# One transformer layer in split fp32: a smaller constant of exponents, and the left side of SBUF 64 bytes lower

## The chip, the core and the metric

The kernel runs on one core of a Trainium2 chip. The metric is the time of one execution on the device, in microseconds (us); several executions are timed, and their median counts. A second, profiled execution gives the trace from which all rows below are taken.

## What is computed

The reference is one layer of a diffusion backbone over 1024 latent tokens and 256 context tokens, 1024 channels wide, all in fp32. Cut to what matters here:

```
h   = x * (1 + scale1) + shift1                 # scale, shift, gate: silu(c) @ w_mod + b_mod
q_b = rope(qk_rms(h @ w_qb + b, q_norm_g))      # 8 heads of 64
qk_rms(t, g) = t * rsqrt(mean(t*t) + 1e-6) * g  # per head
k_b likewise (2 heads); q_a, k_a without qk_rms
o_a = windowed attention (+-128 tokens and the context, a sink per head)
o_b = global attention over 1024 + 256 keys
y   = (sigmoid(g_a) * (o_a @ w_a) + sigmoid(g_b) * (o_b @ w_b)) @ w_out
x   = LN(alpha * x + gate1 * y)
u   = conv3(modulate(x) @ w_up);  y = (silu(u_gate) * u_val) @ w_down     # 2816 wide
out = LN(alpha * x + gate2 * y)
```

## The kernel before

Products are split. An fp32 matrix is held as a high part (its fp32r rounding) and a low part (the rest), and `mm3` (L92 to L95) forms each product with three matmuls: high by high (L93), high by low and low by high (L94, L95). Nearly all have 512 moving columns; some have 256. On TensorE a matmul has a stationary operand of 128 columns and a moving one of up to 512. `split` makes the two parts: a cast on ACT, VectorE or GpSimd (L85, L87) and a subtraction (L90).

The stages, in the order of time: the query projection of branch B with the modulation (q1acc, to 70 us); the other projections and the gates (acc, g, to about 320 us); the two attentions, unit by unit (s: scores, ptr: transposes, av: values, and b, the branch products, between and behind them, to about 805 us); the output product y with the first normalization and the first columns of u (to 990 us); the up products in a seven-product scheme (a, b, c, d by `up_tile`, 990 to 1370 us); the down products in the same scheme (p, yl, yt, to the end). In the attention and after it the order on TensorE is that of the program's text, partly fixed by hand.

SBUF has two stacks of tiles. The left side begins with constants (`const`), then come `hp` (19 general slots of 4 KB, handed out by `ht` and taken back by `hput`) and, later, `opool` and `post`. The right side holds `ph1` and `hTp` in the first phase, and later `qp`, `att`, `wq` and `za` (the last adds sixteen general slots to those of `hp`). So in the later stages an operand from `ht` may lie on either side, and a weight from the rings `w` (pool `wq`) on the right and `wd` (pool `post`) on the left.

The constants are laid one behind the other, and the last of them is `mhalf` (L118), 24 columns of -0.5, that is 96 bytes a partition. It is the exponent of all reciprocal square roots, which GpSimd takes as a power: for the keys (L303, 2 columns), for two tiles of queries at once (L355 in `qstats`, 16 columns, four times between 70 and 126 us), in the normalizations (L1102, 4 or 2 columns) and in the last one (L1678, 1 column). `pqs` and `nqs`, the scales of the queries, are [128, 8 tiles, 8 heads] in the constant `cvt`; they are read again in the attention of branch B, from 460 us on.

Where tiles lie, by the program's own allocation, as the byte address in a partition modulo 512 (tiles and the pieces of them that matmuls read are a whole number of 512 bytes long, so a pool's tiles share the value):

| tiles | before | after |
|---|---|---|
| `ident`, `identr` and all constants ahead of `mhalf` | unchanged | unchanged |
| left: `hp` slots, `opool` (O), `post` (raw, wd) | 288 | 224 |
| right, first phase: weights, hh, hl | 352 | 352 |
| right, later: q1, q2, ring w, `za` slots, maskr | 480 | 480 |
| right, attention: pth, ptl | 224 | 224 |
| right, attention: p | 96 | 96 |

The moving operand is the activation (hh, B, T, O, mh, pth) in most stages; in q1acc, acc and p it is the weight, and in s the key.

Of the kernel before, what the change touches and what calls it, by code (L numbers as in the profile page):

```python
# [7 lines left out]
F32 = mybir.dt.float32  # L8
R32 = mybir.dt.float32r
AF = mybir.ActivationFunctionType  # L10
ALU = mybir.AluOpType
AX = mybir.AxisListType

P = 128
# [56 lines left out]
def layer_kernel(  # L71
# [6 lines left out]
    nc = tc.nc  # L78
# [20 lines left out]
    def ctile(shape, dt, name):  # L99
        return const.tile(shape, dt, tag=name, name=name)  # L100
# [14 lines left out]
    pqs, nqs = (cvt[:, n * 64:n * 64 + 64].rearrange("p (a b) -> p a b", b=8) for n in (0, 1))  # L115
    onec = ctile([P, 1], F32, "onec")
    onesf = ctile([P, P], F32, "onesf")
    mhalf = ctile([P, 24], F32, "mhalf")  # L118
    nc.vector.memset(onec, 1.0)
    nc.vector.memset(onesf, 1.0)  # L120
    nc.vector.memset(mhalf, -0.5)
# [20 lines left out]
    def hput(*names):  # L142
        for n in names:
            hfree.append(hslot.pop(n))
# [177 lines left out]
    def qpost(br, t):  # L322
        q = qtile(br, t)
        q3 = q.rearrange("p (h d) -> p h d", d=HD)
        if br == 0:
            def r0():
                rope(nc.gpsimd if t % 3 == 2 else nc.vector, q, q, 8, ropec[:, t], ropes[:, t], f"q0_{t}")
            return [r0]
        st = {}

        def s1():
            st["tb"] = ph1.tile([P, 2, HD], F32, tag="tb", name=f"tbq{t}", bufs=4)
            gfold(st["tb"], 0, t, nc.gpsimd)
            if t % 2 == 0:
                qstats(t)

        def s2():
            tb = st["tb"]
            rope(nc.gpsimd if t % 3 == 2 else nc.vector, q, q, 8, tb[:, 0], tb[:, 1], f"q1_{t}")
        return [s1] + [lambda: None] * GAP + [s2]  # L340
# [3 lines left out]
    def qsquare(t):  # L344
        nc.scalar.activation(sqq[t // 2 % 2].rearrange("p a b -> p (a b)"), Q[1, t].rearrange("p a b -> p (a b)"),
                             AF.Square)

    def qstats(t):
        sq = sqq[t // 2 % 2]
        ss, ns = (a[:, t:t + 2].rearrange("p a b -> p (a b)") for a in (pqs, nqs))  # L350
        nc.vector.tensor_reduce(out=ss, in_=sq.rearrange("p a (h d) -> p (a h) d", d=HD), axis=AX.X, op=ALU.add)
        if t + 4 < NT:
            qsquare(t + 4)
        nc.vector.tensor_scalar(out=ss, in0=ss, scalar1=1.0 / HD, scalar2=QK_EPS, op0=ALU.mult, op1=ALU.add)
        nc.gpsimd.tensor_tensor(out=ss, in0=ss, in1=mhalf[:, 0:16], op=ALU.pow)  # L355
        nc.gpsimd.tensor_scalar(out=ns, in0=ss, scalar1=-1.0, scalar2=0.0, op0=ALU.mult, op1=ALU.add)
        if t + 2 == NT:
            hput("sqq0", "sqq1")
# [538 lines left out]
    for u in range(nu + 1):  # L897
# [3 lines left out]
        ss = []  # L901
        if u < nu:
            ss = units[u].score_steps()
# [11 lines left out]
        if u < nu:  # L915
            ss = [units[u].context] + ss
# [898 lines left out]
```

## Time and profile before

| | |
|---|---|
| median of 3 runs | 1580.53 us (1579.97 to 1580.74) |
| profiled execution | 1577.74 us |
| its span, first to last instruction | 1576.0 us |
| TensorE (PE) busy | 1544.8 us, 98% |
| VectorE (DVE) busy | 1190.3 us, 76% |
| ScalarE (ACT) busy | 810.1 us, 51% |
| GpSimd (POOL) busy | 759.5 us, 48% |
| mean granted TensorE clock | 0.998 |

A row of the profile's groups reads: line, engine, operation, output<-inputs, output size<-input size, count | busy us, mean ns of one | idle us of the engine just before them and what ended it. A row of the order of time reads: start us, duration us, engine, line, operation. Matmuls overlap in such rows: one lasts some 390 ns, while the next starts after some 230; the time from start to start is what counts. PEld are the loads of the stationary operand, which run beside matmuls. The chain is the work that ended last, followed back from the end.

### The profile page before, as it was taken

Reading aid. Unit: us, or ns where it says so; the run is one execution under the profiler, and the core shown is the slowest. Engines: PE = TensorE matmul, PEld = TensorE weight load, DVE = VectorE, ACT = ScalarE, POOL = GpSimd, SP = SyncE. Lnnn points to the kernel's source line nnn. Section 1 sums busy time; section 2 is a strip of 40 time slices with the busy share of each in tenths; the row PEclk is TensorE's granted clock in tenths of the full one; section 3 lists DMA queues with packets and bytes.
Section 4 is the critical chain, followed back from the end, with each engine's and each line's share of the span. In section 5 each row is a group of like instructions: output and inputs, shape, how many; then the busy total and the mean of one; then the engine's idle time right before and its main releaser. Section 6 shows DMA issues by size and latency. Waiting matters only on the chain.

```text
span 1576.0 us, 21965 instructions
## 1 busy us (share of the span) xinstructions
PE 1544.8 (98%) x7652; PEld 1267.3 (80%) x7652; DVE 1190.3 (76%) x1751; ACT 810.1 (51%) x1436; POOL 759.5 (48%) x729
## 2 busy tenths in 40 slices
PE   9999999999999999999999999999999999999997
PEld 7888888888877787877787988888888888888886
DVE  7587757548888677888665878888887887646897
ACT  5422224358887667788322673544444444435633
POOL 0374403426666556655323555666676675021053
PEclk9999999999999999999999999999999999999999
DMA  9767663222246555530561223233334446996723
GB/s 379 244 210 266 225 220 105 90 84 68 62 133 152 136 132 131 121 78 18 179 159 42 81 81 134 80 108 112 112 106 111 107 108 171 369 262 205 260 81 107
DMA packets 111873, 229.73 MB, mean 146 GB/s; under 512 B 13489, under 2 KB 27313, under 8 KB 111666
## 3 DMA queue, kind: packets, MB, share of 16 engines
q1 hardware_dynamic: 96464, 199.20, 38.2%
q0 software_dynamic: 10400, 20.19, 8.4%
q10 hardware_dynamic: 4898, 8.94, 1.5%
q8 instruction: 60, 0.98, 0.3%
q14 instruction: 51, 0.42, 0.1%
HBM read 177.09 MB, written 65.87 MB: 154 GB/s over the span
## 4 chain that ended last, share of the span: by engine, by line
PE 85%; DVE 8%; ACT 4%; issue 2%; POOL 1%; DMA 0%; DVEq 0%; SPq 0%; ACTq 0%; POOLq 0%
PE ptr L567 5%; PE g L95 4%; PE p L93 4%; PE g L94 4%; PE g L93 4%; PE p L94 4%; PE p L95 4%; PE b L95 3%; PE b L94 3%; PE b L93 3%; PE s L449 2%; PE av L588 2%; PE c L93 2%; PE d L94 2%; PE a L95 2%; PE s L450 2%
## 5 line engine op out<-in xcount | busy, mean ns | idle before, releaser
L577 DVE TENSOR_TENSOR ptl<-ptr,pth 128x512 fp32r<-128x512 f32 x188 | 124.6, 684 | 28.3 <-ACT pth L576 25.7
L90 DVE TENSOR_TENSOR ld<-rd,hd 128x1024 fp32r<-128x1024 f32 x77 | 97.8, 1284 | 51.2 <-ACT hd L85 47.5
L576 ACT CAST pth<-ptr 128x512 fp32r<-128x512 f32 x188 | 106.6, 589 | 57.7 <-PE ptr L567 31.3
L567 PE MATMUL ptr<-ident,p 128*128 128x128 f32 x816 | 126.9, 278 | 8.9 <-DVE ptl L577 5.8
L462 ACT ACTIVATE p<-p,nm 128x1024 f32<-128x1024 f32 (+2 forms) x128 | 125.3, 981 | 9.0 <-DVE p L495 8.3
L85 ACT CAST hd<-rd 128x1024 fp32r<-128x1024 f32 x77 | 79.6, 1047 | 92.1 <-PE p L95 69.9
L567 PEld LDWEIGHTS ptr<-ident,p 128*128 128x128 f32 x816 | 94.0, 140 | 38.4 <-DVE ptl L577 11.4
L588 PE MATMUL av<-pth,VT 128*128 128x512 f32 x236 | 105.1, 445 | 1.0 <-ACT avs L594 0.5
L93 PE MATMUL p<-hd 128*128 128x512 f32 x264 | 105.3, 399 | 0.0
L94 PE MATMUL p<-ld,hd 128*128 128x512 f32 x264 | 104.3, 395 | 0.0
L95 PE MATMUL p<-hd,ld 128*128 128x512 f32 x264 | 104.0, 394 | 0.0
L95 PE MATMUL g<-hh,wlg 128*128 128x512 f32 x256 | 99.7, 390 | 0.4 <-POOL wlg L90 0.4
L93 PE MATMUL g<-hh,whg 128*128 128x512 f32 x256 | 99.9, 390 | 0.0
L94 PE MATMUL g<-hl,whg 128*128 128x512 f32 x256 | 99.6, 389 | 0.0
L589 PE MATMUL av<-ptl,VT 128*128 128x512 f32 x236 | 97.7, 414 | 2.0 <-POOL ptl L90 1.9
L495 DVE TENSOR_SCALAR_CACHE_REDUCE p<-s,cvt,nmc 128x1024 f32<-128x1024 f32 x64 | 84.4, 1339 | 12.6 <-PE s L450 12.4
L90 POOL TENSOR_TENSOR wlg<-wg,whg 128x512 fp32r<-128x512 f32 x32 | 45.1, 1416 | 99.0 <-ACT whg L85 86.2
L449 PE MATMUL s<-KL,q 128*128 128x512 f32 (+2 forms) x192 | 76.2, 397 | 2.7 <-ACT p_x L462 2.0
L87 POOL TENSOR_SCALAR pth<-prw 128x512 fp32r<-128x512 f32 x48 | 31.4, 654 | 87.1 <-ACT prw L573 61.5
L450 PE MATMUL s<-KL,q 128*128 128x512 f32 (+2 forms) x192 | 71.7, 374 | 1.0 <-DMA q<-q 0.9
L85 ACT CAST wA<-ru 128x512 fp32r<-128x512 f32 x57 | 35.4, 621 | 66.7 <-PE d L95 36.3
L85 ACT CAST wS<-s 128x512 fp32r<-128x512 f32 x76 | 45.3, 621 | 46.9 <-POOL s L1148 46.0
(406 smaller groups left out, 4958.0 us busy)
## 6 DMA issues: line engine op xcount, KB each, us to landing
wml<-in_wmodT_dram SPq DMA_DIRECT2D x48, 512.0 KB
ru<-in_w_up_dram SPq DMA_DIRECT2D x38, 512.0 KB
rd<-td SPq DMA_DIRECT2D x55, 256.0 KB
rd<-sd SPq DMA_DIRECT2D x44, 256.0 KB
rd<-in_w_dn_dram SPq DMA_DIRECT2D x33, 256.0 KB
wm<-in_wmodT_dram SPq DMA_DIRECT2D x16, 512.0 KB
wg<-in_w_g_dram SPq DMA_DIRECT2D x32, 256.0 KB
sgd<-sg ACTq DMA_DIRECT2D x32, 256.0 KB
```

What stands on the lines that cost most here:

```text
L85: cast[:] = [nc.scalar.copy(hi, src).ins]
L90: low[:] = [lo_eng.tensor_tensor(out=lo, in0=src, in1=hi.bitcast(F32), op=ALU.subtract).ins]
L93: nc.tensor.matmul(ps, a[0], b[0], start=start, stop=False, skip_group_check=resumed)
L94: nc.tensor.matmul(ps, a[0], b[1], start=False, stop=False, skip_group_check=resumed)
L95: nc.tensor.matmul(ps, a[1], b[0], start=False, stop=stop, skip_group_check=resumed)
L449: nc.tensor.matmul(o, self.q[0][:, hs], ks, start=True, stop=False)
L450: nc.tensor.matmul(o, self.q[1][:, hs], ks, start=False, stop=stop)
L462: nc.scalar.activation(p, s, AF.Exp, bias=nm[:, h:h + 1], scale=scale, accum_out=sm[:, h:h + 1])
L567: nc.tensor.transpose(tr[:, h * P:(h + 1) * P], self.pslice(h, n), ident)
L576: nc.scalar.copy(hi, tr)
L577: nc.vector.tensor_tensor(out=lo, in0=tr, in1=hi.bitcast(F32), op=ALU.subtract)
L588: nc.tensor.matmul(self.av, v, hi, start=first, stop=False)
```

## The change

The constant `mhalf` keeps 8 of its 24 columns. The power of two query tiles needs 16, so it now reads the 8 columns twice, by a broadcast with step 0 over the two tiles; its first operand and its output are written as [128, 2, 8] instead of [128, 16], the same elements in the same order. The other users read at most 8 columns and are as before. The constant is 64 bytes shorter, and every tile above it on the left side lies 64 bytes lower. The right side does not move. On each engine the instructions, their order and their waits are the same.

```diff
@@ -115,7 +115,7 @@
     onec = ctile([P, 1], F32, "onec")
     onesf = ctile([P, P], F32, "onesf")
-    mhalf = ctile([P, 24], F32, "mhalf")
+    mhalf = ctile([P, 8], F32, "mhalf")
     nc.vector.memset(onec, 1.0)
     nc.vector.memset(onesf, 1.0)
     nc.vector.memset(mhalf, -0.5)
@@ -352,7 +352,8 @@
         nc.vector.tensor_scalar(out=ss, in0=ss, scalar1=1.0 / HD, scalar2=QK_EPS, op0=ALU.mult, op1=ALU.add)
-        nc.gpsimd.tensor_tensor(out=ss, in0=ss, in1=mhalf[:, 0:16], op=ALU.pow)
+        nc.gpsimd.tensor_tensor(out=pqs[:, t:t + 2], in0=pqs[:, t:t + 2],
+                                in1=mhalf.unsqueeze(1).to_broadcast([P, 2, 8]), op=ALU.pow)
         nc.gpsimd.tensor_scalar(out=ns, in0=ss, scalar1=-1.0, scalar2=0.0, op0=ALU.mult, op1=ALU.add)
```

## The prediction, written before the changed kernel ran

> **What bounds the kernel now.** I read the page first, for the busy shares and the chain that ended last.
>
> ```profile
> PE 1544.8 (98%) x7652; PEld 1267.3 (80%) x7652; DVE 1190.3 (76%) x1751; ACT 810.1 (51%) x1436; POOL 759.5 (48%) x729
> PE 85%; DVE 8%; ACT 4%; issue 2%; POOL 1%; DMA 0%; DVEq 0%; SPq 0%; ACTq 0%; POOLq 0%
> L93 PE MATMUL p<-hd 128*128 128x512 f32 x264 | 105.3, 399 | 0.0
> L93 PE MATMUL g<-hh,whg 128*128 128x512 f32 x256 | 99.9, 390 | 0.0
> ```
>
> TensorE is the bound: 98% busy and 85% of the chain. The last two rows are the same instruction on the same shape, three-term fp32r products of 512 columns, and yet one takes 399 ns and the other 390. Matmuls overlap, so what the kernel pays is the time from one start to the next, the step. The busy time by stretch gives its mean (columns: stretch, its length, busy time and count of PE, PEld, DVE, ACT, POOL, the granted clock, DMA share, GB/s).
>
> ```profile
> 130.00:250.00 120.00, 120.00 (x531) 99.36 (x530) 78.22 (x131) 29.41 (x50) 32.45 (x26) 1.00 0.64 223
> 470.00:760.00 290.00, 278.68 (x1584) 223.73 (x1583) 229.65 (x397) 213.83 (x470) 174.73 (x241) 1.00 0.48 111
> 805.00:905.00 100.00, 99.61 (x533) 84.64 (x532) 63.27 (x88) 38.28 (x54) 36.79 (x29) 1.00 0.32 91
> 905.00:990.00 85.00, 84.84 (x441) 71.97 (x440) 70.22 (x95) 47.98 (x74) 45.86 (x34) 1.00 0.30 100
> 990.00:1370.00 380.00, 380.00 (x1641) 307.66 (x1640) 311.96 (x275) 178.64 (x244) 235.98 (x134) 1.00 0.46 135
> 1375.00:1505.00 130.00, 130.00 (x559) 104.69 (x558) 89.64 (x89) 64.84 (x70) 23.73 (x19) 1.00 0.82 244
> ```
>
> A matmul lasts nearly two steps, so a count holds some two matmuls that began before its stretch. In the projections and gates (130 to 250) the step is 120 / 529 = 226.8 ns, in the up products (990 to 1370) 380 / 1639 = 231.9, in the down products (1375 to 1505) 130 / 557 = 233.4. TensorE is busy all of the time and the clock is 1.00 in all three, so the 5 to 7 ns are no wait for another engine and no throttle. What differs is where the operands lie. The program's addresses, taken modulo 512 bytes: right side tiles of the first phase 352, left side 288, right side later 480, but pth and ptl 224. I call the moving operand's address less the stationary one's the distance. The order of time shows steps by distance.
>
> ```profile
> 199.70 0.39 PE L93 MATMUL g<-hh,whg 128*128 128x512 f32 x1
> ...
> 201.97 0.39 PE L94 MATMUL g<-hl,whg 128*128 128x512 f32 x1
> ```
> ```profile
> 847.44 0.39 PE L93 MATMUL y<-mh,hwo 128*128 128x512 f32 x1
> ...
> 849.48 0.39 PE L93 MATMUL y<-mh,hwo 128*128 128x512 f32 x1
> ```
> ```profile
> 816.25 0.39 PE L93 MATMUL y<-mh,hwo 128*128 128x512 f32 x1
> ...
> 818.12 0.39 PE L95 MATMUL y<-mh,lwo 128*128 128x512 f32 x1
> ```
> ```profile
> 474.38 0.39 PE L589 MATMUL av<-ptl,VT 128*128 128x512 f32 x1
> ...
> 475.78 0.40 PE L589 MATMUL av<-ptl,VT 128*128 128x512 f32 x1
> ```
> ```profile
> 776.82 0.39 PE L94 MATMUL b<-O,hwb 128*128 128x512 f32 x1
> ...
> 778.65 0.39 PE L93 MATMUL b<-O,hwb 128*128 128x512 f32 x1
> ```
> ```profile
> 1449.79 0.40 PE L93 MATMUL p<-hd 128*128 128x512 f32 x1
> ...
> 1451.89 0.40 PE L93 MATMUL p<-hd 128*128 128x512 f32 x1
> ```
>
> In turn: g, both at 352, distance 0: 10 steps, 2.27 us, 227 ns. y with mh and hwo both on the left at 288, distance 0: 9 steps, 2.04 us, 227 ns. y with mh on the right and hwo on the left, distance 192: 8 steps, 1.87 us, 234 ns. av, 224 against 288, distance -64: 6 steps, 1.40 us, 233 ns. b, 288 against 480, distance -192: 8 steps, 1.83 us, 229 ns. p, which changes between 0, 192 and -192: 9 steps, 2.10 us, 233 ns. The two y pieces are one stage, one loop and the same engines beside it; only the slot differs. So the step follows the distance. Distance 0 is fastest whether both lie at 352 or at 288, so neither place by itself matters. 192 and -64 are the same modulo 256 and cost the same (234 and 233), which I take to mean that the pattern repeats every 256 bytes.
>
> **The change, part by part.** The built program keeps every instruction, its order and every wait; the constant's memset shrinks, the four powers read their second operand through a broadcast, and tiles above the constant on the left come 64 bytes lower, from 288 to 224 modulo 512.
>
> The shift. Now the left is at 224, the later right at 480, pth and ptl at 224: every distance of a 512-column matmul between these tiles becomes 0 or 256 modulo 512, that is 0 modulo 256. If that repeats the distance 0, all of these settle at 226.8 ns.
> - Up products: 1639 x (231.9 - 226.8) = 8.4 us. No other engine is near: DVE works 311.96 of 380.
> - Down products: 557 x (233.4 - 226.8) = 3.7 us in 130 us, so 4.1 for the 145 us from 1370 to 1515. The DMA share there rises from 0.82 to 0.84, still below 1.
> - 805 to 990: by the loops, y has 12 groups and u 9 of 24 matmuls with 512 columns, 504, and some 90 stand at the edges. Runs at 227 and at 234 are about as frequent; I take 4.4 ns over the floor, 594 x 4.4 = 2.6 us. A quarter of the chain here is the normalization on ACT, DVE and POOL, so 1.9 on the path.
> - 470 to 805: the 472 av, and s and b.
>
> ```profile
> L588 PE MATMUL av<-pth,VT 128*128 128x512 f32 x236 | 105.1, 445 | 1.0 <-ACT avs L594 0.5
> by line: PE ptr L567 15.5%; PE av L588 7.9%; PE av L589 7.4%; PE s L449 7.3%; PE s L450 6.8%; DVE ptl L577 6.6%; DVE p L495 6.2%; PE b L93 5.0%; PE b L95 4.8%; PE b L94 4.8%; issue 4.0%; ACT p_x L462 3.6%; ACT p L462 3.2%; ACT pth L576 3.1%
> ```
>
>   The mean of 445 ns, where a dense one takes some 395, says that many of these steps end in a pause; I count half of the 472 at 6.6 ns, 1.6 us. Of s and b some 450 are dense at 229 to 234, at 4 ns 1.8. The chain of 470 to 760 (second row) is broken by others: the PE lines named sum to 60%, so 0.6 x 3.4 = 2.0 us.
> - Around it, 320 to 470 and after 1515, where the chain is mostly waits: 0.3 us.
> - 256-column matmuls go the other way:
>
> ```profile
> 891.89 0.28 PE L93 MATMUL y<-mh,hwo 128*128 128x256 f32 x1
> ...
> 892.58 0.28 PE L93 MATMUL y<-mh,hwo 128*128 128x256 f32 x1
> ...
> 893.51 0.28 PE L95 MATMUL y<-mh,lwo 128*128 128x256 f32 x1
> ...
> 894.36 0.29 PE L93 MATMUL y<-mh,hwo 128*128 128x256 f32 x1
> ```
>
>   From the right at distance 192, 6 steps take 0.69 us, 115 ns; at distance 0, 7 steps take 0.85, 121 ns (both rounded). With equal distances they all settle at the upper value. The mean now is about in the middle; by the loops 192 of y and 144 of u have 256 columns, 336 x 2 ns: -0.7 us.
>
> Sum: 8.4 + 4.1 + 1.9 + 2.0 + 0.3 - 0.7 = 16.0 us less. If another engine were late next it would be DVE, which in the up products would be at 312 of 372, or the loads of the down products at 0.84; neither reaches the whole.
>
> The power. POOL's rows, the four powers and the nearest ones with and without a broadcast operand:
>
> ```profile
> L355 POOL TENSOR_TENSOR cvt<-cvt,mhalf 128x16 f32<-128x16 f32 x4 | 15.0, 3744 | 9.5 <-DVE cvt L354 9.5
> L280 POOL TENSOR_TENSOR rt1q<-Q,tbq 128x512 f32<-128x512 f32 x2 | 2.8, 1382 | 0.0
> L288 POOL TENSOR_TENSOR Q<-rt1q,rt2q 128x512 f32<-128x512 f32 x4 | 6.3, 1563 | 0.2
> L1102 POOL TENSOR_TENSOR rsa<-rsa,mhalf 128x2 f32<-128x2 f32 x2 | 1.5, 756 | 12.0 <-DVE rsa L1100 12.0
> 70.00:130.00 60.00, 60.00 (x266) 49.67 (x266) 51.10 (x80) 16.39 (x26) 42.54 (x35) 1.00 0.68 237
> ```
>
> The rotation at L280 reads its second operand by the same kind of broadcast and takes 1382 ns, no more than the plain addition at L288 with 1563. So I take 0, between 0 and one more start of a small power, 756 ns, for each of four. Behind a power stand its negation and the gate's low parts; POOL is idle 17 of the 60 us of that stretch and TensorE never, so POOL hides it. Were that cover gone, it would cost 4 x 0.76 = 3 us.
>
> The memset and the transfers.
>
> ```profile
> L121 DVE MEMSET mhalf<- x1: 78/78/78, 1.0 to 1.0; 128x24 f32 x1
> ```
>
> The memset lasts 78 ns at the start, so its smaller form saves 0 to 78 ns; I take 0. Transfers to left tiles now land 64 bytes lower; no row splits them by address, so by bounds: the share of the DMA engines is at most 0.82 where TensorE is always busy, and a transfer could last 1.2 times as long before it set the pace. I take 0.
>
> The Trainium skill, "SBUF — State Buffer", section "SBUF: two separate sides", says that on the engine side only the port pair shared by GpSimd and VectorE contends and that TensorE never waits on anyone. By it the distance could not matter and the sum would be 0. The trace does not agree: 227 against 234 ns in one loop.
>
> The profiled execution took 1577.74 us (span 1576.0); less 16.0 is 1561.7. The median of the runs is 2.8 us above the profiled one, so I forecast 1564.5 us.
>
> **The rivals.**
> 1. Only 512 bytes repeat, and 256 is a distance of its own of middling price. The trace holds no 512-column matmul at 256; for it stands only that 192 and -64, which are 256 apart, agree. With the 229 ns of b as its price, the up products gain 1639 x 2.9 = 4.7 us, the down products 2.7, the rest (3.5 above) in the same share 1.9: 9.3 less, 1571.2.
> 2. The distance is not the cause, and slow steps belong to the late stages as such (their rings, their loads). Then nothing moves: 1580.5. Against it: the two y pieces. The skill's rule above would give this time too.
> 3. Slower: 256 is the worst distance. The longest step that returns in the up products is this one:
>
> ```profile
> 1224.07 0.40 PE L94 MATMUL d<-T24l,wA 128*128 128x512 f32 x1
> 1224.31 0.39 PE L95 MATMUL d<-T24h,wA 128*128 128x512 f32 x1
> ```
>
>    240 ns. In the built program 2259 matmuls of 512 columns would lie at 256. If they took 240 instead of about 231.9, 2259 x 8.1 = 18.3 us, nine tenths of it on the path: 16.5 more, 1597. It decides as soon as the mean step of the up products passes 231.9. For it: with 256 columns it is the equal distance that is slow, so no distance is good by nature.
>
> **How the numbers follow.** Forecast 0.75; rival 1 0.09; rival 2, and a power that loses its cover, 0.08; rival 3 0.08. The forecast's own case runs from 1557 (nothing discounted: 8.4 + 4.1 + 2.6 + 3.4 + 1.0 = 19.5, and as an estimate 4 more for waits that shrink along) to 1569 (the up and down products alone, 12.5, less the 0.7); the range goes up to 1574 to take in rival 1, and holds 0.8. About 0.2%, 3.2 us, is what a measurement of this kernel can tell from no change. Faster by more: 0.75 + 0.09 = 0.84; within: 0.08; slower: 0.08.
>
> **What would show it.** Right: a count of about 1677 matmuls in 380 us of up products, p rows at 390 instead of 399 ns, av steps of 227, and 256-column steps of 120. Wrong: a step above 229 in the up products, or a faster TensorE whose gain returns as waits for ACT or DVE before p or ptr. The four powers should stay near 3.7 us.

## The result, and the profile after

| | before | changed |
|---|---|---|
| median of 4 runs each | 1580.63 us (1579.97 to 1581.35) | 1563.18 us (1562.52 to 1568.22) |
| ratio | | 0.9896, 95% interval 0.9875 to 0.9918 |
| profiled execution | 1577.74 us, span 1576.0 | 1568.22 us, span 1566.4 |

The changed kernel is faster by 1.0%; 1564.5 us had been forecast. The two profiled executions stand on opposite sides of their medians: that of before 2.9 us under, that of the changed kernel 5.0 us over. Their spans differ by only 9.6 us, the medians by 17.4. A second trace at the old addresses (experiment 2) accounts for 5.3 of the 7.8 us between them, so the stages come first.

The busy time of each stretch, in the changed kernel (the columns are those of the prediction: stretch and its length, busy time and count of each engine, granted clock, DMA share, GB/s):

```profile
core 0: us, PE busy (x) PEld busy (x) DVE busy (x) ACT busy (x) POOL busy (x), PEclk, DMA share, GB/s
130.00:250.00 120.00, 120.00 (x531) 99.38 (x530) 77.96 (x128) 29.36 (x50) 32.36 (x25) 1.00 0.65 223
805.00:905.00 100.00, 99.27 (x521) 84.78 (x520) 63.27 (x79) 35.62 (x51) 36.76 (x28) 0.98 0.33 94
905.00:990.00 85.00, 84.96 (x454) 73.43 (x454) 69.95 (x101) 48.45 (x74) 45.26 (x34) 1.00 0.29 101
990.00:1370.00 380.00, 380.00 (x1678) 314.73 (x1678) 320.62 (x285) 184.66 (x254) 232.84 (x134) 1.00 0.46 139
```

The projections and gates keep 120 / 529 = 226.8 ns a step (the count includes up to two matmuls that reach over an end of the stretch). In the up products the 380 us hold 1678 matmuls, where they held 1641 before: 380 / 1676 = 226.7 ns. TensorE is still busy all of the time, and DVE, next in line, has 320.62 of 380. So in this stage the matmuls follow one another faster, with no wait gone and none added.

The groups of the changed kernel: the down products, av, the 256-column y, and the four powers with the constant's memset.

```profile
L93 PE MATMUL p<-hd 128*128 128x512 f32 x264 | 103.2, 391 | 0.0
L95 PE MATMUL p<-hd,ld 128*128 128x512 f32 x264 | 102.7, 389 | 0.0
L589 PE MATMUL av<-pth,VT 128*128 128x512 f32 x236 | 104.8, 444 | 1.1 <-ACT avs L595 0.5 <-ACT pth L577 0.3
L93 PE MATMUL y<-mh,hwo 128*128 128x256 f32 x64 | 18.1, 283 | 0.0
L355 POOL TENSOR_TENSOR cvt<-cvt,mhalf 128x16 f32<-128x16 f32 x4 | 15.0, 3742 | 9.5 <-DVE cvt L354 9.5
```
```profile
L121 DVE MEMSET mhalf<- x1: 65/65/65, 1.0 to 1.0; 128x8 f32 x1
```

A p lasts 391 or 389 ns instead of up to 399. av barely moves (444; it was 445). The powers, now with a broadcast operand, take 3742 ns each as against 3744. The memset is 13 ns shorter. The 256-column matmuls of y now all step alike, 47 of them in the 5.64 us between these rows, 120 ns each, as forecast:

```profile
899.77 0.28 PE L93 MATMUL y<-mh,hwo 128*128 128x256 f32 x1
...
905.41 0.28 PE L95 MATMUL y<-mh,lwo 128*128 128x256 f32 x1
```

### The profile page after: what moved, and what is told of

Read it like the earlier page. It is cut to its first block, busy times and chain, and to the rows that moved or that the text cites. A ratio compares the mean times of both kernels' runs of the same rounds, so it can differ in the third digit from the quotient of the medians.

```text
span 1566.4 us, 21965 instructions
## 1 busy us (share of the span) xinstructions
PE 1532.0 (98%) x7652; PEld 1269.8 (81%) x7652; DVE 1195.9 (76%) x1751; ACT 809.0 (52%) x1436; POOL 754.8 (48%) x729
## 4 chain that ended last, share of the span: by engine, by line
PE 86%; DVE 8%; ACT 3%; issue 2%; POOL 1%; DMA 0%; DVEq 0%; ACTq 0%; POOLq 0%
PE ptr L568 5%; PE g L95 4%; PE g L94 4%; PE g L93 4%; PE p L95 4%; PE p L93 4%; PE p L94 4%; PE b L95 3%; PE b L94 3%; PE b L93 3%; PE s L450 2%; PE av L589 2%; PE c L93 2%; PE d L93 2%; PE a L93 2%; PE a L95 2%
```

## The experiments

"Theory" is the prediction's: the step of 512-column matmuls follows the distance between the addresses of its two operands, with period 256. Its rivals 1 to 3 are the prediction's: 256 is a place of its own (1), the late stages as such are slow (2), 256 is the worst distance (3). More rivals were named on the way. Kernels that run chains alone (1, 5 and 8) are timed by one trace each: a chain's step is the time from its first start to the first start of the next chain, divided by the count. In the map's table and its text the time from a chain's first start to its last is divided by the 47 steps between; the two differ by at most 0.2 ns.

### 1. A map of the distance, with TensorE alone

```diff
+    def chain(name, cols, pairs, n=48):
+        o = tile_(name)
+        for i in range(n):
+            s, m = pairs[i % len(pairs)]
+            s, m = s // 4 + 128 * (i % 3), m // 4 + 512 * (i % 2)
+            nc.tensor.matmul(o[:, 0:cols], st[:, s:s + 128], mv[:, m:m + cols], start=i == 0, stop=i == n - 1)
...
+    for d in range(0, 512, 32):
+        chain(f"d{d}x", 512, [(0, d)])
```

> Leaves the whole layer out: it only runs chains of 48 matmuls back to back on TensorE, with no other engine at work, and stores one of the results. Within a chain the moving operand lies d bytes above the stationary one, modulo 512: d from 0 to 480 in steps of 32, with 512 columns and then with 256; six chains repeat d = 0, 128 and 192 with both operands 64 or 160 bytes higher; three have d = 4, 8, 16; and in the last ones the operands alternate between two places, so that the distance to a matmul's own weights and the distance to the next matmul's weights differ. Theory (the step follows the distance, with period 256): with 512 columns about 227 ns at d = 0 and at 256, 229 to 236 at 64 and 192, and the same at 320 and 448; with 256 columns about 113 to 115 at 192 and 120 at 0 and 256; the same step at one d wherever both lie. Rival 1 (256 is a place of its own): 229 or more at 256. Rival 2 (late stages, not addresses): one step for all d. Rival 4 (the place of the left side as such): the chains with both operands 64 or 160 bytes higher differ from those at 0, and d alone does little.

The stretches from the start of one chain to the start of the next, in the order d = 0, 32, 64, 192, 256, 320 with 512 columns, then d = 0 and 64 with 256 columns:

```profile
68.21:79.09 10.88, 10.88 (x50) 9.01 (x48) 0.00 (x0) 0.00 (x0) 0.00 (x0) 1.00 0.00 0
79.09:90.29 11.20, 11.20 (x49) 9.00 (x48) 0.00 (x0) 0.00 (x0) 0.00 (x0) 1.00 0.01 1
90.29:101.29 11.00, 11.00 (x50) 9.02 (x48) 0.00 (x0) 0.00 (x0) 0.00 (x0) 1.00 0.00 0
134.94:146.13 11.19, 11.19 (x49) 9.02 (x48) 0.00 (x0) 0.00 (x0) 0.00 (x0) 1.00 0.01 1
157.32:168.21 10.89, 10.89 (x50) 9.01 (x48) 0.00 (x0) 0.00 (x0) 0.00 (x0) 1.00 0.00 0
179.41:190.41 11.00, 11.00 (x50) 9.01 (x48) 0.00 (x0) 0.00 (x0) 0.00 (x0) 1.00 0.00 0
246.44:252.19 5.75, 5.75 (x50) 5.75 (x49) 0.00 (x0) 0.00 (x0) 0.00 (x0) 1.00 0.00 0
257.85:263.50 5.65, 5.65 (x50) 5.65 (x49) 0.00 (x0) 0.00 (x0) 0.00 (x0) 1.00 0.00 0
```

The same chains by groups, which give each chain's name; s64d0x has d = 0 with both operands 64 bytes higher:

```profile
L101 PE MATMUL d192x<-mv,st 128*128 128x512 f32 x48 | 11.4, 395 | 0.0
L101 PE MATMUL s64d192x<-mv,st 128*128 128x512 f32 x48 | 11.4, 395 | 0.0
L101 PE MATMUL d320x<-mv,st 128*128 128x512 f32 x48 | 11.2, 392 | 0.0
L101 PE MATMUL s64d0x<-mv,st 128*128 128x512 f32 x48 | 11.1, 390 | 0.0
L101 PE MATMUL d256x<-mv,st 128*128 128x512 f32 x48 | 11.0, 389 | 0.0
L101 PE MATMUL d0x<-mv,st 128*128 128x512 f32 x48 | 11.0, 389 | 0.0
```

The steps of all chains with 512 columns, from the starts in the trace:

| distance modulo 256 | 0 | 32 | 64 | 96 | 128 | 160 | 192 | 224 |
|---|---|---|---|---|---|---|---|---|
| d below 256, ns | 226.7 | 233.4 | 229.1 | 233.6 | 233.4 | 234.1 | 233.2 | 233.1 |
| d from 256, ns | 226.8 | 233.4 | 229.1 | 233.6 | 233.4 | 234.1 | 233.2 | 233.1 |

The two rows agree within 0.1 ns: the pattern has a period of 256 bytes, and 256 is as good as 0. Rivals 1 and 3 fall. With both operands moved by 64 or 160 bytes the step is 227.3 and 227.5 for d = 0, and 233.2 for 192. The excess over 226.7 is in the first steps behind the move (229, 231, 230, 236, 229, 232, 231 with 64 bytes); the last 30 of each chain take 226.7, so the place alone does not matter. Distances of 4, 8 and 16 bytes already cost (236.5, 231.5, 231.7). With 256 columns the order is reversed but small, and not clean: 119.7 ns at 0 and 117.9 at 64, but 119.8 at 96; the expected 113 to 115 at 192 was too low (117.8).

The last chains let the operands alternate between two places. Where the own distance is in turn 64 and -64 (192 modulo 256), and the next matmul's weights are always at distance 0, the step is 231.2, just the mean of 229.1 and 233.2; with 128 and -64 in turn it is 233.3, again the mean of the single prices. One chain shows more than the theory had: with the own distance always 0, but the place of both operands moved to and fro by 64 bytes from one matmul to the next, the step is 231.7 instead of 226.7. There the weights of the next matmul, loaded beside this one's stream, lie at 64 or -64. Whether it is these weights or the change of place at every matmul that costs, this chain does not tell; experiment 5 says more.

### 2. The broadcast alone

```diff
     mhalf = ctile([P, 8], F32, "mhalf")
+    ctile([P, 16], F32, "pad")
```

> The changed kernel with a pad of 64 bytes behind the constant: the power still reads eight columns by a broadcast, but every left tile lies where it lay before. Theory (distance): all of the gain is lost, 1580.6 us, within 0.1%. Rival 5 (the power read by a broadcast, or the shorter constant, brings the gain): 1563.2.

Measured: 1581.19 us (before, on the same chip, 1581.15), ratio 0.9999 (0.999 to 1.0008). The gain is gone with the shift; rival 5 falls. The stretches of this kernel:

```profile
805.00:905.00 100.00, 99.83 (x516) 84.29 (x515) 62.16 (x76) 35.57 (x49) 37.59 (x28) 0.98 0.34 90
905.00:990.00 85.00, 84.83 (x455) 72.59 (x455) 70.05 (x103) 48.07 (x73) 44.27 (x34) 1.00 0.32 106
990.00:1370.00 380.00, 380.00 (x1641) 307.74 (x1640) 315.04 (x279) 179.64 (x248) 238.99 (x135) 1.00 0.44 130
```

The up products hold 1641 matmuls as in the kernel before. This trace also settles most of what was missing. It has the old addresses, and its profiled execution took 1583.02 us, 5.3 more than that of before. The table gives the time between the starts of the same matmuls in the traces, in us:

| stage (in the kernel before) | before | broadcast alone | changed | changed less broadcast alone |
|---|---|---|---|---|
| 1 to 130 | 129.03 | 129.93 | 129.79 | -0.14 |
| 130 to 320, projections, gates | 189.94 | 189.94 | 189.94 | 0.00 |
| 320 to 470 | 150.67 | 152.18 | 152.18 | 0.00 |
| 470 to 805, attention | 334.49 | 336.11 | 335.07 | -1.04 |
| 805 to 990, y and u | 184.80 | 186.01 | 184.93 | -1.08 |
| 990 to 1370, up products | 380.22 | 380.22 | 371.73 | -8.49 |
| 1370 to 1515, down products | 144.79 | 144.79 | 140.79 | -4.00 |
| after 1515 | 51.08 | 51.08 | 50.90 | -0.18 |
| sum | 1565.01 | 1570.27 | 1555.35 | -14.92 |

At the same addresses four stages are 0.9 to 1.6 us longer with the broadcast alone than in the trace of before, and the first two of them are as long in the changed kernel; the trace of before is one of the shorter executions. One such piece can be seen: in the changed kernel's trace, matmuls of y are stretched to 0.63 us, at a granted clock of 0.57. The trace of the broadcast alone has the like at the same place (second of the stretches below), the trace of before has not (1.00 there).

```profile
862.22 0.39 PE L95 MATMUL y<-mh,lwo 128*128 128x512 f32 x1
...
863.15 0.63 PE L95 MATMUL y<-mh,lwo 128*128 128x512 f32 x1
863.58 0.63 PE L93 MATMUL y<-mh,hwo 128*128 128x512 f32 x1
```
```profile
862.50:866.50 4.00, 4.00 (x12) 3.14 (x11) 1.37 (x3) 0.00 (x0) 1.03 (x1) 0.57 0.00 0
862.00:867.00 5.00, 5.00 (x21) 4.19 (x21) 1.86 (x6) 0.00 (x0) 1.03 (x1) 0.66 0.00 0
```

The step there is 430 ns instead of 227; the seven matmuls of 0.63 us make 1.4 us. Like with like, the shift is worth 14.9 us in the traces, and 15.4 between the medians of experiments 2 and 3. The 17.4 between the first medians is more than that, but its interval (0.9875 to 0.9918, some 13 to 20 us) holds both; that remainder is not explained.

### 3. The shift alone

```diff
-    onec = ctile([P, 1], F32, "onec")
     onesf = ctile([P, P], F32, "onesf")
-    mhalf = ctile([P, 24], F32, "mhalf")
-    nc.vector.memset(onec, 1.0)
+    onec = onesf[:, 0:1]
+    mhalf = ctile([P, 16], F32, "mhalf")
```

> The kernel before, with the plain power over sixteen columns, and 64 bytes saved otherwise: the constant has sixteen columns instead of twenty-four, and the column of ones is a view of the square of ones instead of a tile of its own (one memset less). The left tiles lie at 224 modulo 512. Theory (distance): the whole gain, 1563.2 us, within 0.2%. Rival 5: 1580.6.

Measured: 1565.75 us, ratio 0.9905 (0.989 to 0.9919), an interval that holds the 0.9896 of the changed kernel. Its up products:

```profile
990.00:1370.00 380.00, 380.00 (x1677) 314.59 (x1677) 319.44 (x285) 184.26 (x253) 231.22 (x134) 1.00 0.46 139
```

1677 matmuls, 226.9 ns. The addresses make the gain; neither the broadcast nor the size of this constant as such has a part in it that these runs can tell.

### 4. The late right side moved after the left

```diff
+    zpad = tc.alloc_tile_pool(name="zpad", bufs=1, side="right", reuse_waits="tile")
+    zpad.tile([P, 16], F32, tag="pad", name="pad")
     za = tc.alloc_tile_pool(name="za", bufs=1, side="right", reuse_waits="tile")
...
     za.release()
+    zpad.release()
```

> The changed kernel with a pad of 64 bytes on the right side from the end of the attention on: left tiles stay 64 bytes lower, but right tiles of the output projection, of the up and of the down products move by 64 bytes, so 1763 matmuls of 512 columns and 224 of 256 return to the distances of before (64 or 192 modulo 256); nothing changes up to the attention. Theory (distance): the late terms of the prediction come back, 8.4 + 4.1 + 1.9 - 0.7 = 13.7 us, so 1576.9 us, between 1575 and 1580; about 232 ns a step in the up products. Rival 4 (the place of the left side as such): 1563.2, since the left stays.

Measured: 1580.69 us, ratio 0.9996 (0.9988 to 1.0005). That lies outside the 1575 to 1580 expected. The expectation left the attention's gain in place, forecast at 2.0 us; in the traces this kernel is 0.5 us shorter there than the broadcast alone (335.57 against 336.11). Some more lies in the base: 1563.2 was taken for the changed kernel, and beside these runs the same shift measured 1565.75 (experiment 3). The stretch of the up products, and the groups of p with the two highest means:

```profile
990.00:1370.00 380.00, 380.00 (x1641) 308.18 (x1641) 318.18 (x279) 179.47 (x248) 239.88 (x135) 1.00 0.44 130
```
```profile
L93 PE MATMUL p<-hd 128*128 128x512 f32 x264 | 105.4, 399 | 0.0
L95 PE MATMUL p<-hd,ld 128*128 128x512 f32 x264 | 104.1, 394 | 0.0
```

The left side lies where the changed kernel has it, and yet the up products are back at 1641 matmuls and take 380.22 us between the starts of the same matmuls, to the hundredth what they took before. Only the distance is as before. The place of the left side as such (rival 4) falls, and with it any cost of transfers that land 64 bytes lower.

### 5. Replay of the kernel's addresses, with TensorE alone

```diff
+    chain("upoldx", 512, UPOLD, 252)
+    chain("upnewx", 512, UPNEW, 252)
+    chain("downoldx", 512, DOWNOLD, 264)
...
+    chain("avnewx", 512, AVNEW, 96)
```

> Leaves the whole layer out: only TensorE chains without any other engine at work. Six of them replay, back to back, the addresses modulo 512 of both operands as the 512-column matmuls of three stages have them in the kernel before (old) and in the changed one (new): 252 matmuls of the up products, 264 of the down products, 96 of av. Four chains have 384 and four have 128 columns at d = 0, 64, 128, 192; two change every six matmuls between d = 0 and d = 128 or 192. Theory (the addresses alone make the whole difference): up old 231.9 ns a step and new 226.8, as the kernels have them with all engines at work; down old 233.4, new 226.8; av old about 233, new 226.8. Rival 6 (the addresses set off a part only, and the other engines and the transfers of those stages add to it): the old chains stay near what the single distances of the map would give, (138 x 226.7 + 72 x 229.1 + 42 x 233.2) / 252 = 228.5 for up, and (226.7 + 229.1 + 233.2) / 3 = 229.7 for down. No expectation for the sizes 384 and 128 but that d = 64 or 192 is not better by more than 3 ns.

The stretches of the six chains: up old, up new, down old, down new, av old, av new.

```profile
67.73:126.08 58.35, 58.35 (x254) 47.30 (x253) 0.00 (x0) 0.00 (x0) 0.00 (x0) 1.00 0.00 1
126.08:183.22 57.14, 57.14 (x254) 47.30 (x252) 0.00 (x0) 0.00 (x0) 0.00 (x0) 1.00 0.00 1
183.22:244.81 61.59, 61.59 (x266) 49.60 (x265) 0.00 (x0) 0.00 (x0) 0.00 (x0) 1.00 0.00 1
244.81:304.65 59.84, 59.84 (x266) 49.55 (x264) 0.00 (x0) 0.00 (x0) 0.00 (x0) 1.00 0.00 1
304.65:327.05 22.40, 22.40 (x98) 18.05 (x96) 0.00 (x0) 0.00 (x0) 0.00 (x0) 1.00 0.00 1
327.05:348.85 21.80, 21.80 (x98) 18.02 (x97) 0.00 (x0) 0.00 (x0) 0.00 (x0) 1.00 0.00 0
```

Divided by 252, 264 and 96: up 231.5 and 226.7, down 233.3 and 226.7, av 233.3 and 227.1 ns. In the kernel, with all engines and the transfers at work, up and down were 231.9 and 233.4 before, and up is 226.7 now. So the addresses alone give 4.8 of the 5.2 ns in up, and in down 6.6, all of the excess; rivals 2 and 6 fall. The old chains are also above what the single distances of the map average to (228.5 and 229.7): changing between distances costs more than each of them held.

The starts within the old chains show why a price for each matmul does not do. In the old down chain every matmul's next weights lie at distance 0, and every third matmul has its own distance 0 too: from its start to the next are 236.0 ns, from the others, at 64 and 192, 231.9 and 232.0. In the old up chain 124 of the 252 matmuls have both at 0, and step at 231.2; the second, third and fourth of such matmuls in a row still take 231.8, 230.6 and 230.3. So equal addresses of a matmul, and of the weights next to come, are not enough for the low step: what ran before counts as well.

With 384 columns the step was 173.6, 173.2, 175.8 and 174.7 at d = 0, 64, 128 and 192, with 128 columns 110.6, 111.7, 111.6 and 111.7; the two chains that change every six matmuls between 0 and 128 or 192 took 231.2 and 231.6, where the mean of the prices held would be 230.

### 6 and 7. Other distances in the whole kernel

```diff
     mhalf = ctile([P, 24], F32, "mhalf")
+    ctile([P, 16], F32, "pad")
...
     mhalf = ctile([P, 8], F32, "mhalf")
+    ctile([P, 8], F32, "pad")
```

Above the dots stands the edit of 6, to the kernel before; below them that of 7, to the changed kernel.

> The kernel before with a pad of 64 bytes behind the constant: left tiles lie 64 bytes higher, at 352 modulo 512, so that all distances that were 64 or 192 modulo 256 become 128. Theory (the map carries over): 128 costs 233.4 ns alone, where 64 costs 229.1 and 192 233.2; with 72 and 42 of 252 matmuls of the up products at these, that is 1.3 ns more a matmul, 2.1 us in the up products, and 1.0 us in the down products: 1584 us, slower by 0.2%. Rival 1 (a period of 512, with 128 a place of its own) or a rule that only tells 0 from all others: the same as before, 1581. Rival 7 (any higher place of the left side is worse in proportion): more than 1590.

> The changed kernel with a pad of 32 bytes behind the constant: left tiles lie at 256 modulo 512, 32 bytes lower than in the kernel before and 32 higher than in the changed one, distances 32 or 224 modulo 256. Theory (the map carries over): 233.4 and 233.2 ns alone, so as with the distance 128: 1584 us. Rival 8 (nearness to 0 is what counts, in proportion to the distance): half way, 1572.

Measured: 1578.73 us, ratio 0.999 (0.9979 to 1.0), for 128, and 1579.88, ratio 0.9998 (0.9988 to 1.0007), for 32 and 224. The forecast of 1584 is missed in both: the prices of the map do not add up in a stream that changes between distances. The up products, distance 128 first and then 32:

```profile
990.00:1370.00 380.00, 380.00 (x1645) 308.60 (x1644) 313.71 (x279) 180.42 (x249) 239.47 (x136) 1.00 0.44 130
```
```profile
990.00:1370.00 380.00, 380.00 (x1640) 307.57 (x1639) 313.56 (x278) 178.84 (x245) 237.77 (x134) 1.00 0.44 131
```

1645 and 1640 against 1641 before. Between the same matmuls the up products took 379.11 and 380.50 us, the down products 143.45 and 143.79 (before 380.22 and 144.79). Rivals 7 (worse in proportion) and 8 (half way, 1572) fall. Of the four placements of the left side that were run, one has all these distances at 0 and gains; the three others lie within 0.1% of each other.

### 8. Short runs

```diff
+        for i in range(96):
+            s, m = 128 * (i % 3), d // 4 + 512 * (i % 2)
+            nc.tensor.matmul(o, st[:, s:s + 128], mv[:, m:m + 512], start=i == 0, stop=i == 95)
+            if i % n == n - 1:
+                nc.tensor.matmul(z[:, 0:128], st[:, 384:512], mv[:, b // 4:b // 4 + 128], ...)
```

> Leaves the whole layer out: only TensorE chains without any other engine at work. Each chain has 96 matmuls of 512 columns at d = 0 or 192, with one matmul of 128 columns put in after every 2, 3, 6, 12 or 24 of them, as the transposes stand between the short runs of av; two pairs of chains with runs of 3 put that small matmul at distance 192 or 64 instead of 0. Theory (the step settles at its low value only some matmuls after a break, which is why av, in runs of 2 or 3, gained less than forecast): at d = 0 the steps inside runs of 2 and 3 are 231 to 234 ns, in runs of 24 on average below 229; at d = 192 about 233 for all lengths; so 0 to 2 ns between the two distances in the short runs, over 4 in the long ones. Rival 9 (av gains less because of the other engines' traffic in that stage): with TensorE alone 227 at d = 0 in runs of any length, 6 ns below d = 192.

The stretches of six chains, in pairs of d = 0 and d = 192: a break after every 3, 12 and 24.

```profile
123.92:149.64 25.72, 25.72 (x130) 21.59 (x129) 0.00 (x0) 0.00 (x0) 0.00 (x0) 1.00 0.00 1
149.64:175.46 25.82, 25.82 (x131) 21.64 (x129) 0.00 (x0) 0.00 (x0) 0.00 (x0) 1.00 0.00 1
223.50:246.38 22.88, 22.88 (x106) 18.93 (x105) 0.00 (x0) 0.00 (x0) 0.00 (x0) 1.00 0.00 1
246.38:269.61 23.23, 23.23 (x106) 18.94 (x105) 0.00 (x0) 0.00 (x0) 0.00 (x0) 1.00 0.00 1
269.61:291.93 22.32, 22.32 (x102) 18.46 (x101) 0.00 (x0) 0.00 (x0) 0.00 (x0) 1.00 0.00 0
291.93:314.75 22.82, 22.82 (x103) 18.50 (x101) 0.00 (x0) 0.00 (x0) 0.00 (x0) 1.00 0.00 1
```

For 96 matmuls, d = 0 wins 0.10 us in runs of 3, 0.06 in runs of 6, 0.35 in runs of 12, 0.50 in runs of 24, and nothing in runs of 2 (27.65 against 27.62 us). By position in the runs of 24 the steps at d = 0 are, from the first on: 284, 229, 235, 230, 232, 231, 227, and 227 from there; at d = 192: 284, 229, 231, 233.5, and 233 from there. A stream comes into step only some six matmuls after a break. In a run of 2 to 6 the distance makes next to no difference yet: at most 1 ns a matmul, against 5.2 in runs of 24. Rival 9 (227 ns at d = 0 in runs of any length) falls, since TensorE was alone and the short runs did not reach it. With the small matmul at distance 192 or 64 instead of 0, d = 0 wins 0.22 us in runs of 3.

## Why the prediction was right, step by step

- **Up products, -8.4 us forecast, -8.49 measured.** 1678 matmuls where about 1677 were named. That the addresses do it, and nothing else that the change touches, is shown by experiments 2 to 5.
- **Down products, -4.1 forecast, -4.00 measured** (down to 226.7 ns in the replay). In the trace of experiment 3 it is 3.2 (141.57 us); a matmul of the normalization's sums (stb) waits 0.3 us for DVE there, and the part after 1515 is 0.9 us shorter (50.01). The transfers did not become the bound: TensorE is busy for all of the 130 us from 1375 to 1505 in the changed kernel, at a DMA share of 0.80.
- **805 to 990, -1.9 and the 256-column matmuls +0.7, together -1.2 forecast, -1.08 measured.** Both sizes were a little high, and the errors work against each other. Where runs at 227 and 234 are as frequent, their mean lies 3.5 ns over the floor, not the 4.4 taken; in dense stretches y with 512 columns went from 230.6 to 227.0 and u from 231.6 to 227.3. With 256 columns y went from 118.1 to 120.0 and u from 118.4 to 119.9: the fast end is 118, not 115, and in the stage this cost 0.43 us.
- **470 to 805, -2.0 forecast, -1.04 measured: the mis-sized term.** The prediction "counted half of the 472" av at 6.6 ns each, 1.6 us and, with its factor of 0.6, about 1.0; in the traces (changed against broadcast alone) the av steps of this stage give 0.14. The b and s gave 1.04, where 0.6 x 1.8 = 1.1 had been put down, and the 120 score matmuls of 256 columns, which the prediction left out, cost 0.13. Steps of 227 were expected in av. But most runs of av between transposes have one or two matmuls (143 of 196 in the kernel). In the trace the step from the second matmul of a run to the third still takes 232.2 ns at the new addresses, and from the third to the fourth 233.8 (before 232.2 and 234.1); only the next one, 229.0, is clearly lower (before 232.8, each without one that waits). Experiment 8 shows the same with TensorE alone, and experiment 5 that a long chain of the same addresses does reach 227. The prediction took the step for a property of the pair of operands; it is one of the stream.
- **Around it, -0.3 forecast, -0.32 measured** (0.14 + 0.18), too little to tell from chance; the forecast gave no working for it.
- **The power and the memset, 0 forecast, 0 measured.** 3742 against 3744 ns, ratio 0.9999 with the broadcast alone. The upper bound of 756 ns for one more start was not touched.
- **Transfers to left tiles, 0 forecast.** Experiment 4 has them lower too, at 1580.69 us.
- **The rivals.** 256 is no place of its own and not the worst distance (experiment 1); the late stages are not slow as such (experiments 4 and 5). The rule of the Trainium skill, "SBUF — State Buffer", section "SBUF: two separate sides", by which TensorE never waits on anyone, gave 0; these runs don't speak for or against waits on another engine, but show that with no other engine at work the step still depends on where TensorE's own two operands lie, by 2 to 10 ns with 512 columns. What in the reading of the operands makes it so, no run here shows.
- **The base.** The forecast added 2.8 us to the profiled execution. Without that step it would have been 1561.7; the median is 1563.18, and the range 1557 to 1574 held it either way. That the forecast came within 1.3 us of the median is in part luck: 16.0 us of gain were forecast, 14.9 stand in the traces and 15.4 between experiments 2 and 3, and the two first medians happened to lie 17.4 apart.

## What to carry to other kernels

Where TensorE is busy all of the time and a stage's count of matmuls per us is below that of another stage at the same clock, compare the addresses of the two operands modulo 256 bytes, over the whole stream and not for each matmul by itself: here a shift of 64 bytes is worth 1%. Place whole pools, on both sides of SBUF, at equal addresses modulo 256, and recheck after any change of a small constant, since that shifts everything behind it. Expect the gain in long uninterrupted streams of 512-column fp32r matmuls only; the 256-column ones lost a little here.

## What the runs showed of the hardware

- A stream of 512-column fp32r matmuls, each with its weight load, steps at 226.7 ns if all moving and stationary operands in it lie equal modulo 256 bytes, and at 229 to 237 if moving and stationary operands differ, even by only 4 bytes (236.5).
- The pattern repeats after 256 bytes within 0.1 ns, and the place of the pair as such does not move the settled step (226.7 in the last 30 matmuls at all three places tried).
- With 256 columns equal places are among the slower ones, 119.7 to 119.9 against 117.8 to 119.8 elsewhere; with 384 and 128 the spread is 2.6 and 1.1 ns.
- A stream reaches its low step only some six matmuls after a break. The replayed streams of the kernel before and those that change every six matmuls stay at 231 to 233 ns, above the mean of their single prices (228.5 to 230).
- Single executions of one kernel differ by up to 8 us (the kernel before beside experiments 1 to 4: 1577.67 to 1585.41), in waits and in a dip of the granted clock to 0.57 over 4 us. So the difference of two profiled spans (9.6 us) was no measure of the change (15 to 17).
